# Four edits in the first mixer and the attention of a two-block transformer: a sign step, the input splits, nine modulation columns, and the log-sigmoid rows

## The chip, the cores and the metric

The kernel runs on one core of a Trainium2 chip. The metric is the device time of one execution in microseconds, lower being better. The kernel before takes 2660.37 us (median of 3 runs, 2654.53 to 2660.7).

## The reference, cut to what matters

Two blocks follow each other on a sequence of 512 tokens with 1024 channels. The first block is a stack of two layers, each a mixer and a convolutional gated MLP, with adaptive norms: a vector c gives shift, scale and gate of every norm by a product with a 1024 x 3072 matrix (the "modulation"). The second block is not touched by the change. All is float32.

```python
def adaln_params(c, w, b):                     # shift, scale, gate: 3 x 1024 values
    mod = jax.nn.silu(c) @ w + b
def s5_mixer(h, ...):                          # layer 0
    u = h @ w_in                               # 64 groups of 16 channels, 64 complex states each
    ...                                        # per group: y = scan(bu, lb) through c_re, c_im
    y = jax.nn.gelu(y + d_skip * u)
    y = y * jax.nn.sigmoid(y @ w_glu)
    return y @ w_out
def fox_mixer(h, ...):                         # layer 1, 16 heads
    log_f = jax.nn.log_sigmoid(f_logit + b_f)
    F = lax.cumsum(log_f)                      # one row of 512 per head
    s = q @ k.T + F[t] - F[s]                  # causal, then softmax and p @ v
```

## The kernel before

Channels lie on partitions in eight tiles of 128 x 512 tokens. Each float32 product is three matmuls of rounded halves: high by high, low by high, high by low (`mm3`, L378 to L380). ScalarE (ACT) writes a weight's high half `whi` (L271), VectorE (DVE) or GpSimd (POOL) the low half `wlo` (L272).

**The S5 mixer** takes the first 337 us. Its 64 groups are handled as eight tables of eight groups. For each table n there are steps, each with a letter, and the string ORDER (L76 to L84) writes out by hand in which order they are emitted, and so the order on each of PE, ACT, DVE and POOL; the order on SP's queue, which issues the DMAs, is settled by a list scheduler. W splits an input weight; G is its product with the modulated input, whose result goes out to DRAM (`ud`); F, C, K, R and U build the table (R the rotations on DVE, L924 to L926, C the output weights on POOL, L957 to L959, U two DMAs that turn the rotations into `ecs`); u puts a sign on half of `ecs` (ACT, L987) and writes the decay factors `d` (L990); P transposes (L997, copied to `bp` on ACT, L998); Q makes the lag products (L1006, L1009, copied to `lags` on ACT); A copies them to a Toeplitz tile T with eight DMAs; L loads `ud` back as U; I is the input product (L1027) with two ACT copies (L1030); S multiplies by `ecs`, scans (DVE, L1037 to L1040), copies the halves across (ACT, L1043) and forms `w1` (DVE, L1045); B is L1051 and L1052 on DVE; O the output product (L1060 with T, L1062 with `w1`), a gelu on ACT into `dg` and a DMA to DRAM (`yd`). Y loads `yd` back and splits it into halves, v splits a GLU weight, a and b are GLU matmuls. A round of ORDER, as I call a line of it, has S of table n, P and Q of table n+1, I of table n+1 and O of table n.

**The start.** `split_x(k)` writes the modulated input `hnh` (ACT, L891) and `hnl` (ACT L895 or DVE L893, then DVE L896) of a channel tile. Two of the eight stand ahead of the table powers (`lf`, DVE rows of L721 with ACT copies of L1085 and L1092 between them); the other six are merged among these.

**Modulation columns.** A column of 128 outputs is one 512 KB DMA into a buffer `ada` (L135, two buffers in turn) and one multiply with a sum on DVE (L136). After 16 or 8 columns a bias is added (L151). Columns wait in a list; during a product one or two at a time are taken off at a rate per matmul group, and `need(key)` takes off all that are still before a key's sum. Before the change the list begins behind ORDER, with the 8 gate columns of S5, then 24 for the next norm (`f0`). The eight `z` products after it (`project_out`) apply the gate (L446), and at channel tile 6 of 8 the next norm's `need("f0")` comes.

**The attention of layer 1.** The cumulative sums Fc (16 x 512) are negated to `nF` in two halves, and for each head a matmul with a selector column spreads its row over 128 partitions (L1354), ACT copies it to `b` (L1356), and POOL adds the causal mask to give `bd` (L1358). `scores` adds them to the products on DVE (L575, L578).

Of the kernel before, what the change touches and what calls it, by code (L numbers as in the profile page):

```python
# [9 lines left out]
F32 = mybir.dt.float32  # L10
F32R = mybir.dt.float32r
I32 = mybir.dt.int32
AF = mybir.ActivationFunctionType
OP = mybir.AluOpType
# [4 lines left out]
P = 128  # L19
D = 1024  # L20
S = 512
KD = D // P
# [6 lines left out]
C1 = 6.28125  # L29
C2 = 0.0019350051879882812  # L30
C3 = TWO_PI - C1 - C2
# [21 lines left out]
def _consts():  # L53
# [19 lines left out]
C_DVE, BC_BUFS = 0, 3  # L73
Z_POOL, W_ADD, SUMS_POS, SPREAD_POS, GATE_RATE = 0, 'dve', 12, 22, 1.3
T_ACT, MERGE_AT = 0, 50
ORDER = ("W1 G0 W2 G1 F0 L0 P0 K1 R0 U0 U1 W3 G2 Q0 A0 C1 F1 L1 I0 u0 K2 "  # L76
# [8 lines left out]
LAG_BUFS, U_BUFS, U_ACT, W_DVE, LO_POOL, BC_POS, XR, NORM_POOL, V_DVE, SP_ORDER = 2, 3, 0, 0, 0, 4, 0, 8, 0xaa, 2  # L85
EARLY = 6
BG_AT, BG_RATE = 0, 1.3
# [4 lines left out]
def tile_two_blocks(ctx, tc, ap, out):  # L92
    nc = tc.nc
# [19 lines left out]
    def col(name, i=0, n=1):  # L113
        return vec[:, _OFF[name] + i:_OFF[name] + i + n]
# [7 lines left out]
    def bcast_load(name):  # L122
        t = cst.tile([P, D], F32, name="cb")
        src = ap[name]
        nc.sync.dma_start(t, bass.AP(tensor=src.tensor, offset=src.offset, ap=[[0, P], [1, D]]))
        act.activation(t, t, AF.Silu)
        return t
# [17 lines left out]
    def ada(name, first, cb, m, bias, key, n=24):  # L145

        items = ada_items(name, first, n, cb, m)
        for part, a, b in (("", 0, min(16, n)), ("gate", 16, n)):
            if a < b:
                def done(a=a, b=b, part=part):  # L150
                    dve.tensor_add(m[:, a:b], m[:, a:b], bias[:, a:b])  # L151
                    finished.add(key + part)
                background.extend(items[a:b] + [done])
# [8 lines left out]
    def bg(n):  # L162
        for _ in range(min(n, len(background))):
            background.pop(0)()
# [212 lines left out]
    def mm3(ps, wh, wl, xh, xl, start, stop):  # L377
        pe.matmul(ps, wh, xh, start=start, stop=False)  # L378
        pe.matmul(ps, wh, xl, start=False, stop=False)  # L379
        return pe.matmul(ps, wl, xh, start=False, stop=stop).ins  # L380
# [24 lines left out]
    def bg_rate(r):  # L405
        tick[0] = r
        tick[1] = 0.0
# [315 lines left out]
    def merge(*lists):  # L723

        todo = sorted(((i + 0.5) / len(l), n, i) for n, l in enumerate(lists) for i in range(len(l)))
        for _, n, i in todo:
            lists[n][i]()

    with tc.block(schedule_with_timeline_sim=TIMELINE):
# [156 lines left out]
        def split_x(k):  # L886
            hi, lo = hnp.tile([P, S], F32R, name="hnh"), hnp.tile([P, S], F32R, name="hnl")
            X.append((hi, lo))
            a, b = A[:, k:k + 1], B[:, k:k + 1]
            v = tmp.tile([P, S], F32, name=f"t{k % 4}")  # L890
            act.activation(hi, hs[k], AF.Identity, bias=b, scale=a)  # L891
            if V_DVE >> k & 1:
                dve.tensor_scalar(v, hs[k], a, b, op0=OP.mult, op1=OP.add)  # L893
            else:
                act.activation(v, hs[k], AF.Identity, bias=b, scale=a)  # L895
            (pool if LO_POOL >> k & 1 else dve).tensor_tensor(lo, v, hi.bitcast(F32), OP.subtract)  # L896
# [3 lines left out]
        def split_w(n, eng):  # L900
            t = weights(None, D, eng, raws[n])
            if n + 2 < KD:
                raws.append(load_w(n + 2))
            return t
# [128 lines left out]
        def states(tab, sab):  # L1033

            sa, sb = sab
            z0 = tmp.tile([P, G8, 64], F32, name="t0")
            dve.tensor_mul(z0, sa, tab.ec)  # L1037
            dve.tensor_mul(sb, sb, tab.es)
            dve.tensor_tensor(sa, z0, sb, OP.add)
            dve.tensor_tensor_scan(sa.rearrange("p a b -> p (a b)"), tab.d0.rearrange("p a b -> p (a b)"),  # L1040
                                   sa.rearrange("p a b -> p (a b)"), 0.0, OP.mult, OP.add)
            for a in range(2):
                act.activation(sb[HALF[a]], sa[HALF[1 - a]], AF.Copy, scale=-1.0)  # L1043
            w1 = tmp.tile([P, G8, 64], F32, name="t3")
            dve.tensor_mul(w1, sa, tab.ec)  # L1045
            return w1, sb

        def back(tab, wz):
# [19 lines left out]
                              ys.rearrange("p g n -> p (g n)"))  # L1068

        def load_y(i):  # L1070
            if order.index(i) % 2:
                y = tmp.tile([P, 8, 64], F32, name="sq")
            else:
                y = adp.tile([P, D], F32, name="ada")[:, 0:S].rearrange("p (j n) -> p j n", j=8)
            nc.sync.dma_start(y, yd[i].rearrange("j p n -> p j n"))
            return y.rearrange("p j n -> p (j n)")

# [29 lines left out]
        for x, y, z, op in ((KR, kre, kim, OP.subtract), (KI, kim, kre, OP.add)):  # L1107
            sh = [P, NG, 8]
            t = tmp.tile(sh, F32, name="t0")
            pool.tensor_tensor(x, LR[:, :, 0:8], y[:, :, None].to_broadcast(sh), OP.mult)  # L1110
            pool.tensor_tensor(t, LI[:, :, 0:8], z[:, :, None].to_broadcast(sh), OP.mult)
            pool.tensor_tensor(x, x, t, op)
        dve.tensor_tensor(mod00[:, 0:16].rearrange("p (j i) -> p j i", i=4), ada_ps[:, :, 0::32].rearrange("p i j -> p j i"),
                          col("ada_b", 0, 16).rearrange("p (j i) -> p j i", i=4), OP.add)
        A, B = affine(mod00, 0, 8, col("norm_g", 0, KD), "s5")
        split_x(0)
        split_x(1)
        wt = split_w(0, dve)
        tabs[0].for_c(pool)
        merge([lambda k=k: split_x(k) for k in range(2, KD)], lf.ops)  # L1120
        weights_of, sab, wz, w_of, wg = {0: wt}, {}, {}, {}, {}
        tabs, U = [tabs[0]] + [None] * (KD - 1), [None] * KD
        Y, glu = [None] * KD, {}
# [33 lines left out]
        def do_glu(m, i):  # L1157
            if not i:
                glu[m] = ps_mm.tile([P, S], F32, name="mm")
            k = order[i]  # L1160
            cs_ = slice(k * P, (k + 1) * P)
            mm3(glu[m], wg[m][0][:, cs_], wg[m][1][:, cs_], *Y[k], i == 0, i == KD - 1)
        steps = {
            "K": do_tables, "F": lambda n: tabs[n].for_b(dve), "C": lambda n: tabs[n].for_c(dve if C_DVE >> n & 1 else pool),
            "W": do_w, "G": lambda n: gather(n, weights_of.pop(n)), "P": lambda n: tabs[n].on_pe(), "Q": lambda n: tabs[n].for_lags(), "L": do_u,
            "I": do_inputs, "S": do_states, "B": do_back, "A": lambda n: tabs[n].toeplitz(), "O": do_outputs,
# [7 lines left out]
        scope.close()  # L1174
        zp = scope.enter_context(tc.tile_pool(name="zp", bufs=16))
        bg_rate(GATE_RATE)
        cb1 = bcast_load("c")
        ada("ada_w", 0, cb1, mod00[:, 16:24], col("ada_b", 16, 8), "s5", 8)
        mod01 = cst.tile([P, 24], F32, name="m_ada01")
        mod10 = cst.tile([P, 24], F32, name="m_ada10")  # L1180
        ada("ada_w", 8, cb1, mod01, col("ada_b", 24, 24), "f0")
        ada("ada_w", 32, cb1, mod10, col("ada_b", 48, 24), "fox")
        Z = []
        for m in range(KD):
            if m in glu:
# [128 lines left out]
    pool.memset(one, 1.0)  # L1314
    Fc = ap_.tile([16, S], F32, name="Fc", bufs=1)
    dve.tensor_tensor_scan(Fc, one, pl, 0.0, OP.mult, OP.add)
    nF = ap_.tile([P, S], F32R, name="nF", bufs=1)
    pool.memset(nF.bitcast(F32), 0.0)
    act.activation(nF[0:16], Fc, AF.Copy, scale=-1.0)
    dve.scalar_tensor_tensor(nF[32:48], Fc, -1.0, nF[0:16].bitcast(F32), op0=OP.mult, op1=OP.subtract)  # L1320
    Fq = ap_.tile([P, 4, 16], F32, name="Fq", bufs=1)
    act.activation(Fq, token_major(Fc), AF.Copy)
    sel = ap_.tile([P, 16], F32R, name="sel", bufs=1)
    sel_f = ap_.tile([P, 16], F32, name="sel_f", bufs=1)
    nc.sync.dma_start(sel_f, ap["sel"])
    act.activation(sel, sel_f, AF.Copy)

    mask4 = cc[:, None, 128:256].to_broadcast([P, 4, P])
    Q, K, V = {}, {}, {}
# [1 line left out]
    def qkv_units(wq, wk, wv, X, scale, first):  # L1331
# [16 lines left out]
                units += [lambda i=i, w=wts: uv(i // 2, 0, w), lambda i=i, w=wts: uv(i // 2, 1, w)]  # L1348
        return units

    def fox_head(t, cur):
        i, hh = t // 2, t % 2
        pb = ps_t.tile([P, S], F32, name="pt")
        pe.matmul(pb, sel[:, t:t + 1].to_broadcast([P, P]), nF, start=True, stop=True)  # L1354
        b = tmp.tile([P, S], F32, name="t0")
        act.activation(b, pb, AF.Copy)  # L1356
        bd = tmp.tile([P, S], F32, name="t1")
        pool.tensor_tensor(bd.rearrange("p (a b) -> p a b", a=4), b.rearrange("p (a b) -> p a b", a=4), mask4, OP.add)  # L1358
        cur.scores(Q[i][hh], *K[i][hh], b, bd, 1.0, fq=Fq[:, :, t])
        return V[i // 2]  # L1360

# [359 lines left out]
```

## Time and profile before

| what | value |
|---|---|
| median of 3 runs | 2660.37 us (2654.53 to 2660.7) |
| the profiled execution's own time, and its span | 2663.97 us, 2662.2 us |
| busy time in the span: PE, DVE, ACT, POOL | 2525.7, 1737.6, 1149.0, 359.2 us |
| mean granted clock of TensorE | 0.968 of full |
| PE busy, 102 to 235 us (rounds of S5) | 106.23 of 133 us, clock 0.75 |
| PE busy, 330 to 350 us (end of S5 to the MLP) | 11.92 of 20 us, clock 0.66 |
| PE busy, 740 to 965 us (attention) | 209.19 of 225 us, clock 1.00 |

Busy time of PE alone does not tell where time is lost: at half clock a matmul counts as busy for longer. So clock and busy time are read together, by stretch.

### The profile page before, as it was taken

What the parts mean: (1) busy time and instruction counts of PE and PEld (TensorE: products, weight loads), DVE (VectorE), ACT (ScalarE), POOL (GpSimd) and SP (SyncE); (2) the same over time, 40 slices, a digit from 0 to 9 for tenths busy, and PEclk for the clock granted to TensorE, in tenths of its full rate; (3) what the DMA queues carried; (4) which work ended last, traced back from release to release, by engine and by line L of the source; (5) the groups of instructions that cost most, each with busy time, mean ns of one, the idle gap of its engine ahead of it and who ended that gap; (6) DMA issues with size and microseconds to landing.
All of it is one profiled execution on the core that took longest, in us unless ns stands there. A gap on an engine that the chain in (4) does not pass through costs nothing. (4 is left out here: it accounts for less than half of the span.)

```text
span 2662.2 us, 32825 instructions
## 1 busy us (share of the span) xinstructions
PE 2525.7 (95%) x12098; PEld 2019.1 (76%) x12098; DVE 1737.6 (65%) x3111; ACT 1149.0 (43%) x1925; POOL 359.2 (13%) x346
## 2 busy tenths in 40 slices
PE   5987999999999999999999999999999889999998
PEld 1776778888867777888887777788888667788887
DVE  8764885455586677546567666975767776753554
ACT  3443353233355554323335554532434576542442
POOL 5550000000031110000022110640000220000000
PEclk7877989999999999999999999999999899999999
DMA  5553654444333334455433323545543103223322
GB/s 208 147 131 115 227 185 133 147 138 123 100 120 97 117 122 160 150 177 179 142 101 115 119 92 127 162 148 170 173 138 99 32 29 96 83 88 99 99 79 75
DMA packets 131120, 335.67 MB, mean 126 GB/s; under 512 B 37008, under 2 KB 41872, under 8 KB 130960
## 3 DMA queue, kind: packets, MB, share of 16 engines
q1 hardware_dynamic: 129232, 331.74, 39.6%
q8 instruction: 95, 1.56, 0.2%
q10 hardware_dynamic: 1728, 1.84, 0.2%
q14 instruction: 65, 0.53, 0.1%
HBM read 320.68 MB, written 6.29 MB: 123 GB/s over the span
## 5 line engine op out<-in xcount | busy, mean ns | idle before, releaser
L272 DVE TENSOR_TENSOR wlo<-wraw,whi 128x1024 fp32r<-128x1024 f32 (+4 forms) x424 | 465.1, 1097 | 419.3 <-ACT whi L271 413.6
L271 ACT ACTIVATE whi<-wraw 128x1024 fp32r<-128x1024 f32 (+4 forms) x431 | 407.9, 948 | 748.9 <-PE mm L379 554.3
L378 PE MATMUL mm<-hnh,whi 128*128 128x512 f32 x1152 | 469.3, 408 | 19.3 <-ACT hnh L317 7.5
L379 PE MATMUL mm<-hnl,whi 128*128 128x512 f32 x1152 | 464.7, 404 | 12.4 <-DVE hnl L896 7.5
L380 PE MATMUL mm<-hnh,wlo 128*128 128x512 f32 x1152 | 460.5, 400 | 3.3 <-DVE wlo L272 3.1
L378 PE MATMUL mm<-g,whi 128*128 128x512 f32 (+1 forms) x922 | 359.7, 391 | 6.3 <-ACT g L271 3.1
L380 PE MATMUL mm<-g,wlo 128*128 128x512 f32 (+1 forms) x922 | 359.2, 390 | 0.0
L379 PE MATMUL mm<-g,whi 128*128 128x512 f32 (+1 forms) x922 | 358.9, 389 | 0.1
L378 PE MATMUL s<-hnh,whi 128*128 128x512 f32 x720 | 288.4, 400 | 0.0
L379 PE MATMUL s<-hnl,whi 128*128 128x512 f32 x720 | 285.4, 396 | 0.0
L380 PE MATMUL s<-hnh,wlo 128*128 128x512 f32 x720 | 284.1, 395 | 0.0
L378 PEld LDWEIGHTS mm<-hnh,whi 128*128 128x128 f32 x1152 | 219.7, 191 | 72.9 <-ACT hnh L317 7.9
L379 PEld LDWEIGHTS mm<-hnl,whi 128*128 128x128 f32 x1152 | 219.8, 191 | 71.4 <-DVE hnl L896 11.3
L380 PEld LDWEIGHTS mm<-hnh,wlo 128*128 128x128 f32 x1152 | 219.5, 191 | 54.3 <-DVE wlo L272 5.1
L136 DVE SCALAR_TENSOR_TENSOR ada<-ada,cb 128x1024 f32<-128x1024 f32 x192 | 239.3, 1247 | 9.7 <-DMA ada<-in_ada_w_dram 9.5
L378 PEld LDWEIGHTS mm<-g,whi 128*128 128x128 f32 x922 | 173.5, 188 | 45.4 <-ACT g L271 3.8
L379 PEld LDWEIGHTS mm<-g,whi 128*128 128x128 f32 x922 | 173.9, 189 | 37.7 <-DVE g L277 0.7
L380 PEld LDWEIGHTS mm<-g,wlo 128*128 128x128 f32 x922 | 173.7, 188 | 37.5 <-issue 0.8
L380 PEld LDWEIGHTS s<-hnh,wlo 128*128 128x128 f32 x720 | 135.2, 188 | 32.7 <-issue 0.7
L378 PEld LDWEIGHTS s<-hnh,whi 128*128 128x128 f32 x720 | 135.4, 188 | 30.3
L379 PEld LDWEIGHTS s<-hnl,whi 128*128 128x128 f32 x720 | 135.5, 188 | 29.9 <-issue 0.5
L591 ACT ACTIVATE p<-p,nb 128x128 f32<-128x128 f32 x192 | 105.6, 552 | 69.8 <-DVE nb L586 41.7
(416 smaller groups left out, 3725.8 us busy)
## 6 DMA issues: line engine op xcount, KB each, us to landing
ada<-in_mod_w_dram SPq DMA_DIRECT2D x96, 512.0 KB, 4.2
wraw<-in_ffn_w_up_dram SPq DMA_DIRECT2D x88, 512.0 KB, 3.6
wraw<-in_f_win_dram SPq DMA_DIRECT2D x88, 512.0 KB, 3.5
ada<-in_ada_w_dram SPq DMA_DIRECT2D x80, 512.0 KB, 4.3
wraw<-in_ffn_w_down_dram SPq DMA_DIRECT2D x32, 384.0 KB, 3.1
wraw<-in_f_wout_dram SPq DMA_DIRECT2D x32, 384.0 KB, 3.1
wraw<-in_ffn_w_down_dram SPq DMA_DIRECT2D x32, 320.0 KB, 2.8
wraw<-in_f_wout_dram SPq DMA_DIRECT2D x32, 320.0 KB, 2.8
```

Source lines behind the costliest of these rows:

```text
L136: dve.scalar_tensor_tensor(raw, raw, 1.0, cb, op0=OP.mult, op1=OP.mult, accum_out=dst[:, i:i + 1])
L271: act.activation(hi, v, AF.Copy)
L272: return eng.tensor_tensor(lo, v, hi.bitcast(F32), OP.subtract)
L378: pe.matmul(ps, wh, xh, start=start, stop=False)
L379: pe.matmul(ps, wh, xl, start=False, stop=False)
L380: return pe.matmul(ps, wl, xh, start=False, stop=stop).ins
L591: act.activation(p[:, sl], p[:, sl], AF.Exp, bias=nb[:, qb:qb + 1], scale=scale, accum_out=l[:, qb:qb + 1])
```

## The change

It has four parts. (1) In ORDER the sign step u(n+1) moves from behind O of a round to ahead of the input copies of the same round, and `w1` of S is written ahead of the two ACT copies. (2) At the start the first weight's split and all eight `split_x` come in a row, the table powers after them. (3) A step c loads and activates c and fills the list of columns in round 5 (the line of S5, run after O5), and nine steps g take the eight gate columns of S5 and their bias add in rounds 6 and 7 of ORDER; `yd` is always loaded into a buffer of the name `sq`. (4) The selector matmul, its ACT copy and the low half of `nF` go; `nF` goes to DRAM and each head's row is read back to all 128 partitions by a DMA, for head t and t+1 when head t is emitted.

```diff
-         "S1 W5 F3 B1 U3 C3 P2 G4 Q2 A2 I2 O1 u2 L3 K4 "
+         "S1 W5 F3 B1 U3 C3 P2 G4 Q2 u2 A2 I2 O1 L3 K4 "
...
-         "S5 F7 B5 U7 C7 P6 Q6 A6 I6 O5 Y0 u6 L7 Y1 v0 "
-         "S6 B6 Y2 P7 Q7 A7 a0 a1 I7 O6 u7 Y3 v1 "
+         "S5 F7 B5 U7 C7 P6 Q6 u6 A6 I6 O5 Y0 L7 c0 Y1 v0 "
+         "S6 g0 B6 Y2 g0 P7 Q7 u7 A7 a0 a1 I7 O6 g0 Y3 v1 g0 "
...
+            w1 = tmp.tile([P, G8, 64], F32, name="t3")
+            dve.tensor_mul(w1, sa, tab.ec)
             for a in range(2):
                 act.activation(sb[HALF[a]], sa[HALF[1 - a]], AF.Copy, scale=-1.0)
-            w1 = tmp.tile([P, G8, 64], F32, name="t3")
-            dve.tensor_mul(w1, sa, tab.ec)
...
+        wt = split_w(0, dve)
...
-        split_x(0)
-        split_x(1)
-        wt = split_w(0, dve)
+        for k in range(KD):
+            split_x(k)
         tabs[0].for_c(pool)
-        merge([lambda k=k: split_x(k) for k in range(2, KD)], lf.ops)
+        merge(lf.ops)
...
+        def do_columns(_):
+            bg_rate(0)
+            c_rows.append(bcast_load("c"))
+            cb1 = c_rows[0]
+            ada("ada_w", 0, cb1, mod00[:, 16:24], col("ada_b", 16, 8), "s5", 8)
...
+            "c": do_columns, "g": lambda n: bg(1),
...
-    nF = ap_.tile([P, S], F32R, name="nF", bufs=1)
...
+    nFd = drp.tile([16, S], F32, name="nFd")
+    nc.sync.dma_start(nFd, nF)
...
+    def load_decay(t):
+
+        b = tmp.tile([P, S], F32, name="t0")
+        nc.sync.dma_start(b, nFd[t:t + 1, :].to_broadcast([P, S]))
+        bd = tmp.tile([P, S], F32, name="t1")
+        pool.tensor_tensor(bd.rearrange("p (a b) -> p a b", a=4), b.rearrange("p (a b) -> p a b", a=4), mask4, OP.add)
+        decay[t] = b, bd
...
-        pb = ps_t.tile([P, S], F32, name="pt")
-        pe.matmul(pb, sel[:, t:t + 1].to_broadcast([P, P]), nF, start=True, stop=True)
-        b = tmp.tile([P, S], F32, name="t0")
-        act.activation(b, pb, AF.Copy)
-        bd = tmp.tile([P, S], F32, name="t1")
-        pool.tensor_tensor(bd.rearrange("p (a b) -> p a b", a=4), b.rearrange("p (a b) -> p a b", a=4), mask4, OP.add)
+        for u in range(t, min(t + 2, 16)):
+            if u not in decay:
+                load_decay(u)
+        b, bd = decay[t]
```

On ACT, in the round of O0 (`lags` are the copies of Q1, `s<-s` those of I1, `dg` is O0's gelu, the rows of L987 and L990 are u1), the difference reads:

```order
 L1011 ACTIVATE lags<-pt 16x512 x2
+L987 ACTIVATE ecs<-ecs,cc 128x512
+L990 ACTIVATE d_125<-sm_mag 128x8x63
 L1030 ACTIVATE s<-s 64x512 x2
 L1065 ACT_TABLE_LOAD
 L1065 ACTIVATE dg<-s 128x512
-L987 ACTIVATE ecs<-ecs,cc 128x512
-L990 ACTIVATE d_125<-sm_mag 128x8x63
 L941 ACTIVATE bc<-bc,cc 128x128
```

The sign now stands ahead of the input copies, no longer behind the gelu, which waits for O0's last matmul. The following rounds show the same move.

On DVE at the end of the S5 stage, the last rows of the output products of the kernel before (L446 writes the residual tiles; the pair L151 and L421 forms the next norm's shift and scale, L318 the low halves of the next input):

```order
L136 SCALAR_TENSOR_TENSOR ada,m_ada_1954<-ada,cb 128x1024
L272 TENSOR_TENSOR wlo<-wraw,whi 128x1024
L190 TENSOR_TENSOR sqa<-sqa,sq 128x512
L136 SCALAR_TENSOR_TENSOR ada,m_ada_1954<-ada,cb 128x1024 x2
L446 SCALAR_TENSOR_TENSOR h_98<-mm,m_ada_132,h_98 128x512
L151 TENSOR_TENSOR m_ada_1954<-m_ada_1954,vec 128x16
L421 SCALAR_TENSOR_TENSOR A_f_2498<-m_ada_1954,vec 128x8
```

and in the changed kernel the rows around the third last residual tile:

```order
L318 SCALAR_TENSOR_TENSOR hnl<-h_94,A_f_2498,hnh 128x512
L318 SCALAR_TENSOR_TENSOR hnl<-h_95,A_f_2498,hnh 128x512
L446 SCALAR_TENSOR_TENSOR h_96<-mm,m_ada_132,h_96 128x512
L272 TENSOR_TENSOR wlo<-wraw,whi 128x1024
L136 SCALAR_TENSOR_TENSOR ada,m_ada_606<-ada,cb 128x1024 x2
L190 TENSOR_TENSOR sqa<-sqa,sq 128x512
L318 SCALAR_TENSOR_TENSOR hnl<-h_96,A_f_2498,hnh 128x512
```

The bias add and the scale, which stood behind the last residual tile, now stand ahead of the third last, and five low halves of the next input with them.

On SP in the attention, the changed kernel's first loads (`nFd` is the copy of `nF` in DRAM, `t` the tiles that take a head's row):

```order
L1324 DMA nFd<-nF 16x512
L360 DMA wraw<-in_fox_w_in_dram 128x1024
L1356 DMA t_5729<-nFd 128x512
L1356 DMA t_5733<-nFd 128x512
L360 DMA wraw<-in_fox_w_in_dram 128x1024
L135 DMA ada<-in_ada_w_dram 128x1024
L1356 DMA t_5809<-nFd 128x512
L360 DMA wraw<-in_fox_wv_dram 128x1024
L1356 DMA t_5934<-nFd 128x512
```

Sixteen such loads and one store are new in this queue; they stand among the weights and columns that it issued before.

## Rows read from the trace of the kernel before

**Rows 1.** By stretch: its us, busy us of PE, PEld, DVE, ACT, POOL, clock, DMA.
```profile
102.00:235.00 133.00, 106.23 (x677) 93.48 (x676) 82.40 (x124) 59.67 (x109) 52.20 (x38) 0.75 0.46 116
330.00:350.00 20.00, 11.92 (x43) 9.37 (x42) 18.34 (x45) 6.86 (x12) 0.00 (x0) 0.66 0.63 230
350.00:720.00 370.00, 369.01 (x1608) 298.89 (x1607) 208.84 (x275) 134.42 (x176) 6.98 (x5) 1.00 0.44 138
```

**Rows 2.** The same view, three rounds of S5.
```profile
102.00:120.00 18.00, 17.24 (x111) 15.17 (x110) 16.25 (x23) 9.42 (x18) 10.44 (x7) 0.81 0.48 126
157.00:173.00 16.00, 14.34 (x114) 12.66 (x113) 10.07 (x18) 9.04 (x18) 10.96 (x9) 0.99 0.61 143
195.00:220.00 25.00, 16.03 (x96) 14.26 (x96) 8.59 (x11) 9.94 (x16) 2.53 (x2) 0.56 0.39 96
```

**Rows 3.** PE in order of time, first matmul of outputs O0 and O4.
```profile
101.67 0.43 PE L1060 MATMUL s<-U,T 128*128 128x64 f32 x2 [1.15 <-DVE t L1052]
172.88 0.69 PE L1060 MATMUL s<-U,T 128*128 128x64 f32 x2 [1.66 <-DVE t L1052]
```

**Rows 4.** Who waited for the sign (L987), and for the copies (L1043).
```profile
  DVE s L1038: 13.0, 3
...
  DVE t L1045: 11.6, 8
```

**Rows 5.** DVE in order of time, a rotation beside POOL and after it.
```profile
103.97 1.54 DVE L926 TENSOR_TENSOR ada<-ada,sqa 128x512 f32<-128x512 f32 x1
107.96 0.69 DVE L926 TENSOR_TENSOR ada<-ada,sqa 128x512 f32<-128x512 f32 x1
```

**Rows 6.** The start in order of time: second weight's low half, second gather's copy.
```profile
67.25 2.37 POOL L272 TENSOR_TENSOR wlo<-wraw,whi 128x1024 fp32r<-128x1024 f32 x1 [8.97 <-ACT whi L271]
78.33 0.60 ACT L911 ACTIVATE sq<-mm 128x512 f32<-128x512 f32 x1 [4.78 <-PE mm L380]
```

**Rows 7.** Rounds 5 to 7 in order of time, ACT, PE and DVE.
```profile
180.00 0.60 ACT L1065 ACTIVATE dg<-s 128x512 f32<-128x512 f32 x1 [7.57 <-PE s L1062]
180.50 0.71 ACT L987 ACTIVATE ecs<-ecs,cc 128x512 f32<-128x512 f32 x1
...
182.96 1.28 ACT L126 ACT_TABLE_LOAD   x1 [0.45 <-DMA cb<-in_c_dram]
...
185.59 1.17 ACT L1043 ACTIVATE s<-s 64x512 f32<-64x512 f32 x2
...
187.41 0.58 PE L1006 MATMUL pt<-cp,bt 128*16 128x128 f32 x2 [5.74 <-ACT bp L998]
...
234.69 0.69 PE L1062 MATMUL s<-t,cp 128*128 128x63 f32 x2 [3.35 <-DVE t L1052]
```

**Rows 8.** End of S5 in order of time.
```profile
329.92 0.39 PE L380 MATMUL mm<-z,wlo 128*128 128x512 f32 x1
334.38 1.23 DVE L136 SCALAR_TENSOR_TENSOR ada<-ada,cb 128x1024 f32<-128x1024 f32 x1 [1.25 <-DMA ada<-in_ada_w_dram]
336.20 0.17 DVE L151 TENSOR_TENSOR m_ada<-m_ada,vec 128x16 f32<-128x16 f32 x1
337.77 0.80 PE L378 MATMUL mm<-hnh,whi 128*128 128x512 f32 x1 [7.46 <-ACT hnh L317]
346.00 0.63 PE L380 MATMUL mm<-hnh,wlo 128*128 128x512 f32 x1
```

**Rows 9.** Attention: selector matmuls, who waits for the mask add, and the first score.
```profile
L1354 PE MATMUL pt<-nF,sel x16: 392/398/507, 761.3 to 944.4; 128*128 128x512 f32 x16
...
  DVE p L578: 8.8, 11
...
762.64 0.29 DVE L575 CUSTOM_DVE_ANT_0 p<-s,t 128x128 f32<-128x128 f32 x1 [0.16 <-ACT t L1356]
```

**Rows 10.** DMA issues of 60 to 260 us: KB each, median us to landing.
```profile
U<-ud SPq DMA_DIRECT2D x8, 256.0 KB, 3.7
T<-lags SPq DMA_DIRECT2D x8, 8.0 KB, 1.8
```

More of the change, by code (lines that the diff above doesn't have):

```diff
@@ L75 @@
 T_ACT, MERGE_AT = 0, 50
-ORDER = ("W1 G0 W2 G1 F0 L0 P0 K1 R0 U0 U1 W3 G2 Q0 A0 C1 F1 L1 I0 u0 K2 "
[8 rows of a table removed]
+ORDER = ("W1 G0 W2 G1 F0 L0 P0 K1 R0 U0 U1 W3 G2 Q0 A0 C1 F1 L1 u0 I0 K2 "
[8 rows of a table added]
 LAG_BUFS, U_BUFS, U_ACT, W_DVE, LO_POOL, BC_POS, XR, NORM_POOL, V_DVE, SP_ORDER = 2, 3, 0, 0, 0, 4, 0, 8, 0xaa, 2
@@ L1070, in load_y @@
         def load_y(i):
[L1071 to L1074, printed above, removed]
+            y = tmp.tile([P, 8, 64], F32, name="sq")
             nc.sync.dma_start(y, yd[i].rearrange("j p n -> p j n"))
@@ L1162, in do_glu @@
             mm3(glu[m], wg[m][0][:, cs_], wg[m][1][:, cs_], *Y[k], i == 0, i == KD - 1)
+        mod01 = cst.tile([P, 24], F32, name="m_ada01")
+        mod10 = cst.tile([P, 24], F32, name="m_ada10")
+        c_rows = []
+        def do_columns(_):
[3 more added lines that the diff above has]
+            ada("ada_w", 0, cb1, mod00[:, 16:24], col("ada_b", 16, 8), "s5", 8)
+            ada("ada_w", 8, cb1, mod01, col("ada_b", 24, 24), "f0")
+            ada("ada_w", 32, cb1, mod10, col("ada_b", 48, 24), "fox")
         steps = {
+            "c": do_columns, "g": lambda n: bg(1),
             "K": do_tables, "F": lambda n: tabs[n].for_b(dve), "C": lambda n: tabs[n].for_c(dve if C_DVE >> n & 1 else pool),
@@ L1176, in tile_two_blocks @@
         bg_rate(GATE_RATE)
[L1177 to L1182, printed above, removed]
+        cb1 = c_rows[0]
         Z = []
@@ L1316, in tile_two_blocks @@
     dve.tensor_tensor_scan(Fc, one, pl, 0.0, OP.mult, OP.add)
-    nF = ap_.tile([P, S], F32R, name="nF", bufs=1)
-    pool.memset(nF.bitcast(F32), 0.0)
-    act.activation(nF[0:16], Fc, AF.Copy, scale=-1.0)
-    dve.scalar_tensor_tensor(nF[32:48], Fc, -1.0, nF[0:16].bitcast(F32), op0=OP.mult, op1=OP.subtract)
+    nF = ap_.tile([16, S], F32, name="nF", bufs=1)
+    act.activation(nF, Fc, AF.Copy, scale=-1.0)
+    nFd = drp.tile([16, S], F32, name="nFd")
+    nc.sync.dma_start(nFd, nF)
     Fq = ap_.tile([P, 4, 16], F32, name="Fq", bufs=1)
     act.activation(Fq, token_major(Fc), AF.Copy)
[L1323 to L1326, printed above, removed]
     mask4 = cc[:, None, 128:256].to_broadcast([P, 4, P])
@@ L1349, in qkv_units @@
         return units
+    decay = {}
+    def load_decay(t):
[4 more added lines that the diff above has]
+        decay[t] = b, bd
     def fox_head(t, cur):
         i, hh = t // 2, t % 2
-        pb = ps_t.tile([P, S], F32, name="pt")
-        pe.matmul(pb, sel[:, t:t + 1].to_broadcast([P, P]), nF, start=True, stop=True)
-        b = tmp.tile([P, S], F32, name="t0")
-        act.activation(b, pb, AF.Copy)
-        bd = tmp.tile([P, S], F32, name="t1")
-        pool.tensor_tensor(bd.rearrange("p (a b) -> p a b", a=4), b.rearrange("p (a b) -> p a b", a=4), mask4, OP.add)
+        for u in range(t, min(t + 2, 16)):
+            if u not in decay:
+                load_decay(u)
+        b, bd = decay[t]
         cur.scores(Q[i][hh], *K[i][hh], b, bd, 1.0, fq=Fq[:, :, t])
```

10 rows, old and new, of the table ORDER are left out of this document.

## The prediction

> **What bounds the kernel now.** I read the busy time and the granted clock by stretch first, since busy time alone hides slow matmuls. In the MLP PE is busy for 369 of 370 us at full clock [rows 1]; nothing that this change touches could shorten that. Two stretches differ: the S5 rounds (106 busy of 133 us at clock 0.75) and the 20 us at the end of S5 (11.9 busy at 0.66). There PE waits, and after waits it runs at the lower of its two levels, 1.2 instead of 2.4 GHz. Then, in those stretches, I read PE and the engines that it waits for in order of time, and who waited for the lines that the change moves. The attention is nearly full (209 of 225 us, table).
>
> The rounds from O0 to O4 are four periods in 172.88 - 101.67 = 71.2 us [rows 3], 17.8 us each. One round that PE ran at full clock (157 to 173 us) holds 14.34 us of PE work [rows 2]. So 3.5 us of every round is idle time or low clock. DVE is the engine waited for at O (1.15 and 1.66 us), and DVE itself waited 13.0 us for the sign in three places and 11.6 us for the cross copies in all eight tables [rows 4].
>
> **Part 1, the sign and w1.** No instruction is added; one ACT pair (0.71 us for L987 [rows 7], 1.3 with the `d` copy behind it) moves from behind the gelu, which waits for O's last matmul, to a place ahead of the input copies, where ACT otherwise waits for PE's input product. What is queued behind it there are those copies; the rotated `ecs` it waits for was issued about a round earlier, so I count no new wait. S of the next table then no longer follows O of this one. Can the round fall to PE's 14.3 us? DVE is busy 16.25 us in a round with rotations and 10.07 in one without [rows 2], 13.2 on average, so DVE fits, though without much to spare, since a rotation round's surplus must be made up in the next. I add 1.1 us per round for the O waits of rows 3, which I take to stay in about that size, and get 15.4 us: 4 x (17.8 - 15.4) = **-9.6 us**. Bounds: 0 (another wait takes the place) and 4 x 3.46 = -13.8 (PE full).
>
> Round 5: PE waits 5.74 us for `bp` before Q6 [rows 7]. This is a chain on ACT: O4's gelu at 180.00, the sign at 180.50, four small table copies, the Silu of c with its table load of 1.28 from 182.96 on, the cross copies at 185.59 (1.17), then `bp`. The Silu and its load hold ACT for 2.3 us of it, the sign pair for 1.3. Without them the scan is done before O4 ends, and everything behind the gelu comes 3.6 to 3.7 us sooner: **-3.7**. Round 6: between two Y splits the sign pair (1.3) leaves and load and Silu (2.3) come, in the same chain to Q7: **+1.0**. Round 7: O7's `w1` wait of 3.35 us [rows 7] hangs on DVE; the sign leaves it (-1.3), one column multiply of 1.23 us [rows 8] enters ahead of S7, and `w1` goes beside the cross copies (-0.6): **-0.6**. The rounds: -12.9.
>
> The Trainium skill gives about 2.7 us for a table load (ScalarE: Activation LUTs, Table sets: the hidden batching unit); by that, round 6 would cost 1.4 us more. The row shows 1.28 us here, and I keep it.
>
> **Part 2, the start.** The first gather waits for low halves of input tiles that are merged among the table powers; with all eight splits in a row it ends earlier. But the second gather needs the second weight, whose high half on ACT stands behind copies that wait for the table powers. Before, POOL waited 8.97 us for that half, split the weight from 67.25 on for 2.37 us, and the gather's copy came at 78.33 [rows 6]. The powers now come after all splits instead of between them, so this half moves little: of the work ahead of it only the waits between splits and powers go. I estimate POOL's split 1.5 us and, with a gather that follows the first one closer, the copy 2.5 us sooner: **-2.5**. Bounds: 0, since the scale of the splits now waits for a weight split of about that 2.37 us ahead of it on DVE, and -9 (POOL's whole wait).
>
> **Part 3, nine columns.** The gate columns cost the same DMAs and 1.23 us multiplies, earlier; on DVE they go where it waited for splits and scans in rounds 6 and 7 (8.6 of 25 us busy from 195 to 220 us [rows 2]). At the end the taking-off at the sum has two entries left instead of nine, and the order shows the bias add three residual tiles earlier. In the trace the last `z` product starts at 329.92 + 0.39 to its end, the next PE work at 337.77 after 7.46 us of waiting [rows 8]; the last wait in it is a column's DMA (1.25 at 334.38) and the add at 336.20. PE then runs at half clock until after 346.00: matmuls of 0.63 us instead of 0.39. Half of these nine us is lost, 4.4 us. With high and low halves of five input tiles ready early, both go: -7.46 - 4.4, and I add back 1 us for the statistics, which now come sooner after the last residual tile: **-10.9** (bounds -12 and -5, the latter if the columns before it still come too late). On SP the third and fourth column, which wait for buffers that the first two free, stand ahead of T7's eight DMAs; I count 2 to 3 us of delay there, and T7 has about 8 us to spare ahead of O7.
>
> **Part 4, the decay rows.** Sixteen selector matmuls go, 0.398 us each, at a spacing of 0.23 us 3.7 us of PE [rows 9]; sixteen ACT copies of 0.6 us beside other work cost nothing either way. Against it: the first head. `nF` is written at 759.6; then a store and a load. The nearest rows are 1.8 us for the smallest copy and 3.7 for 256 KB out of DRAM [rows 10], 5.5 in all, plus issues and 1.3 to 2.6 for the mask: the first score, at 762.64, comes near 768, and PE has projections to do meanwhile for most of that. Later heads have their rows a head ahead, some 13 us, against 3.7 + 1.3; the 8.8 us that DVE waited for the mask go, but not on PE's path. I take 3.7 - 2.7 = **-1.0**, between -5 (waits go too) and +6 (start bare).
>
> **The sum.** -12.9 - 2.5 - 10.9 - 1.0 = -27.3 from the profiled execution's own 2663.97 us: 2636.7. The runs shown have a median 3.6 us below that one, which gives 2633.1. I say **2634 us**; the likeliest case's own range is 2619 to 2646.
>
> **Rivals.**
>
> A. *DVE and POOL hold each other up, and rounds stay long.* The same L926 takes 1.54 us while POOL builds output weights and 0.69 after [rows 5]; POOL is busy 10.4 to 11 us of each round [rows 2]. A shorter round puts more of DVE's work beside POOL's. If the round therefore stays at 17.8, the 9.6 go: 2643. Against it: the odd rounds have 10.07 us of DVE beside the same POOL work. The Trainium skill says that a DVE instruction with two SBUF inputs and a GpSimd one that reads SBUF shut each other out for their whole length (SBUF — State Buffer, Who interferes with whom); the two L926 rows agree in direction, and by that rule A is what a round tends to.
>
> B. *The transition's wait is replaced.* The need that popped nine entries goes, but DVE still waits for column DMAs, or the residual tiles come later behind five low halves (0.7 us each) and PE lacks a free PSUM bank. The 10.9 shrink to 2: 2643. With A: 2652.
>
> C. *The rounds' tail wakes up.* If denser work keeps PE at full clock in rounds 5 and 6 (busy 16 of 25 us at 0.56 [rows 2]), up to 8 us more go: 2626. For it, O4 to Q6 get closer; against, Q7 still waits some 9 us.
>
> D. *Slower: decay rows stuck in SP's queue.* A load issued for head t+1 waits for the buffers of head t-1, and the weights and columns behind it wait too; or it stands behind a weight load that waits for a buffer. If each of the 16 heads then exposes more than (27.3 + 8) / 16 = 2.2 us of PE time, the kernel is slower; with 3 us it is 2634 + 48 = 2682. Against it: the loads are small and a head has 13 us.
>
> E. *The edits don't do what they say*: a sign that waits for its turn DMA ahead of the input copies stalls ACT. A wait of 2.4 us in each of the early rounds cancels the gain there; time as in A, and down to 2660 if B holds too.
>
> **How the numbers follow.** Forecast 0.58, A 0.16, B 0.07, C 0.10, D 0.04, E and mixtures of A and B near no change 0.05. What a measurement of this kernel can tell from no change is about 0.3%, 8 us: under 2652.4 it is faster, over 2668.4 slower. Faster 0.90 (forecast, C, most of A and B), same 0.06, slower 0.04. The range of 8 in 10 goes from 2615 (C with the better bound of the rounds) to 2652 (A with B).
>
> **What would show it.** Right: O0 to O4 in about 62 us; no DVE wait for L987; PE wait before Q6 near 2 us; no wait after the last `z` product and full clock at 340 us; second gather's copy near 76. Wrong: periods still near 18 us with DVE rows of 1.5 us; a DMA wait on DVE in the `z` products; DVE or POOL waiting for decay rows in heads after the second.

## The result, and the profile after

The changed kernel takes 2633.02 us (median of 4 runs, 2630.27 to 2637.51) against 2659.13 us (4 runs) for the kernel before: a ratio of 0.990 with a 95% interval of 0.9886 to 0.9913, so 23 to 30 us faster. The forecast was 2634 us. That the sum came out does not mean that its terms did: two of them were off by nearly 5 us each, in opposite directions, and that they cancel is luck.

The table follows the two profiled executions (spans 2662.2 and 2635.6 us) from mark to mark. A mark is the start of a PE instruction, read from PE's rows in order of time.

| from, to | before, us | after, us | gain, us | forecast, us |
|---|---|---|---|---|
| start to O0 | 101.67 | 98.80 | 2.9 | 2.5 |
| O0 to O4 | 71.21 | 66.40 | 4.8 | 9.6 |
| O4 to O5 | 21.93 | 13.57 | 8.4 | 3.7 |
| O5 to O7's first matmul with w1 | 39.88 | 39.05 | 0.8 | -0.4 |
| that to the end of the last z product | 95.62 | 95.62 | 0.0 | 0 |
| to the transposes of the forget gates (fx) | 426.71 | 416.13 | 10.6 | 10.9 |
| to the last attention product | 203.60 | 199.33 | 4.3 | 1.0 |
| to the end of the span | 1701.6 | 1706.7 | -5.1 | 0 |

The last row holds no code that the change touches. In the fourteen profiled executions of this document (twelve experiments, before and after) this stretch takes 1698.7 to 1708.5 us, so -5.1 lies within the spread of single executions and is no effect of the change that could be told; the profiled execution of the changed kernel was the longest of its four runs.

First the stretches of [rows 1] in the profile after (columns as there):

```profile
102.00:235.00 133.00, 101.53 (x709) 88.08 (x708) 97.17 (x144) 62.71 (x114) 52.20 (x38) 0.85 0.59 158
330.00:350.00 20.00, 19.07 (x85) 14.70 (x85) 19.09 (x23) 14.97 (x22) 6.19 (x4) 1.00 0.42 143
350.00:720.00 370.00, 367.46 (x1613) 295.66 (x1613) 205.69 (x286) 129.57 (x173) 8.41 (x9) 1.00 0.42 132
```

PE is busy for less of the 133 us than before although it does more matmuls there (709 instead of 677): the clock is 0.85 instead of 0.75. DVE now works 97 of these 133 us. The 20 us from 330 on are no longer the end of S5, since the kernel is well ahead there, and they show an undisturbed MLP.

PE's waits from Q1 up to O7's `w1` in the profile after, in order of time, with the starts of O0 to O5 between them (98.80, 119.76, 133.89, 151.06, 165.20, 178.77); two waits of 1.40 and 0.53 us for a GLU weight, behind O6, are left out:

```profile
94.73 0.38 PE L1006 MATMUL pt<-cp,bt 128*16 128x128 f32 x2 [1.67 <-ACT bp L998]
98.80 0.39 PE L1060 MATMUL s<-U,T 128*128 128x64 f32 x2
113.58 0.59 PE L1006 MATMUL pt<-cp,bt 128*16 128x128 f32 x2 [4.65 <-ACT bp L998]
119.76 0.39 PE L1060 MATMUL s<-U,T 128*128 128x64 f32 x2
133.89 0.39 PE L1060 MATMUL s<-U,T 128*128 128x64 f32 x2
147.00 0.38 PE L1006 MATMUL pt<-cp,bt 128*16 128x128 f32 x2 [2.98 <-ACT bp L998]
151.06 0.39 PE L1060 MATMUL s<-U,T 128*128 128x64 f32 x2
165.20 0.39 PE L1060 MATMUL s<-U,T 128*128 128x64 f32 x2
173.35 0.59 PE L1006 MATMUL pt<-cp,bt 128*16 128x128 f32 x2 [3.54 <-ACT bp L998]
178.77 0.39 PE L1060 MATMUL s<-U,T 128*128 128x64 f32 x2
195.17 0.59 PE L1006 MATMUL pt<-cp,bt 128*16 128x128 f32 x2 [11.78 <-ACT bp L998]
217.82 0.69 PE L1062 MATMUL s<-t,cp 128*128 128x63 f32 x2 [4.55 <-DVE t L1052]
```

The waits for t ahead of O0 to O4 of [rows 3] are gone, and no instruction waits for the sign any more ([rows 4] had 13.0 us). But the rounds are unequal: 20.96 us from O0 to O1, then 14.13, 17.17, 14.14. The odd rounds run at PE's speed. The two longer ones are those with rotations, and the wait in them is for `bp`. Only one of these waits is new, the 4.65 us ahead of Q2. The kernel before had none there, but it waited for `bp` ahead of Q1 (1.05 us), Q4, Q6 ([rows 7]) and Q7:

```profile
151.37 0.38 PE L1006 MATMUL pt<-cp,bt 128*16 128x128 f32 x2 [2.92 <-ACT bp L998]
212.52 0.58 PE L1006 MATMUL pt<-cp,bt 128*16 128x128 f32 x2 [8.97 <-ACT bp L998]
```

ACT, DVE and POOL in the first of the long rounds after tell why:

```profile
101.17 1.53 DVE L926 TENSOR_TENSOR ada<-ada,sqa 128x512 f32<-128x512 f32 x1
102.12 1.61 POOL L958 TENSOR_TENSOR op<-LI,bc 128x576 f32<-128x576 f32 x1
102.63 1.65 DVE L924 TENSOR_TENSOR ada<-cb 128x512 f32<-128x512 f32 x1
103.81 1.76 POOL L959 TENSOR_TENSOR cp<-cp,op 128x576 f32<-128x576 f32 x1
104.20 1.92 DVE L925 TENSOR_TENSOR sqa<-cb 128x512 f32<-128x512 f32 x1
106.16 0.69 DVE L926 TENSOR_TENSOR ada<-ada,sqa 128x512 f32<-128x512 f32 x1
...
110.08 0.69 DVE L1043 TENSOR_TENSOR t<-s,ecs 128x512 f32<-128x512 f32 x1
...
110.81 1.17 ACT L1045 ACTIVATE s<-s 64x512 f32<-64x512 f32 x2 [6.44 <-DVE t L1043]
111.91 1.04 ACT L271 ACTIVATE whi<-wraw 128x1024 fp32r<-128x1024 f32 x1
112.85 1.06 ACT L998 ACTIVATE bp<-pt 128x512 f32<-128x512 f32 x2
```

The rotations, beside POOL, take 8.7 us (98.04 to 106.77; about 4.2 alone). Each of the five that meet POOL ends 0.54 or 0.55 us after the POOL instruction that was under way when it began (104.28 after 103.73, 106.12 after 105.57). S1 comes behind them on DVE; the cross copies of S1 wait for it on ACT for 6.44 us, and `bp`, whose transposes PE had ended at 103.4, stands behind those and a weight split. Also, the copies start when `w1` has ended (110.08 + 0.69), not when the scan has.

The end of S5 after, against [rows 8], PE and DVE in order of time:

```profile
297.57 0.17 DVE L151 TENSOR_TENSOR m_ada<-m_ada,vec 128x16 f32<-128x16 f32 x1
...
313.05 0.39 PE L380 MATMUL mm<-z,wlo 128*128 128x512 f32 x1
313.27 0.40 PE L378 MATMUL mm<-hnh,whi 128*128 128x512 f32 x1
313.51 0.40 PE L379 MATMUL mm<-hnl,whi 128*128 128x512 f32 x1
```

The bias add is done 15 us ahead of the last z product, PE goes on without a wait, and at full clock. In the attention, against [rows 9], the first score waits for its row now:

```profile
740.45 0.29 DVE L575 CUSTOM_DVE_ANT_0 p<-s,t 128x128 f32<-128x128 f32 x1 [2.43 <-DMA t<-nFd]
```

It comes 10.88 us after the fx transposes (729.57), where it was 5.62. The view of DMA issues has 1.6 us for the store of `nF` and 3.3 us in the middle for a row.

### The profile page after: what moved, and what is told of

Same layout as the page of the kernel before. It is cut to its first block, busy times and chain, and to the rows that moved or that the text cites. A ratio compares the mean times of both kernels' runs of the same rounds, so it can differ in the third digit from the quotient of the medians.

```text
span 2635.6 us, 32802 instructions
## 1 busy us (share of the span) xinstructions
PE 2506.6 (95%) x12082; PEld 2004.9 (76%) x12082; DVE 1742.7 (66%) x3110; ACT 1140.0 (43%) x1908; POOL 357.5 (14%) x345
## 5 line engine op out<-in xcount | busy, mean ns | idle before, releaser
L478 ACT ACTIVATE t<-t 128x512 f32<-128x512 f32 x88 | 55.5, 631 | 185.9 <-DVE t L455 176.5
```

Source lines behind the costliest of these rows:

```text
L478: act.activation(sa, ya, AF.Silu)
```

## The experiments

All ratios are against runs of the kernel before on the same chip in the same session; the changed kernel's own is 0.9900 (0.9886 to 0.9913). Medians of different sessions differ by a microsecond or two, and the medians of single kernels have 4 to 8 runs, so I read differences under 4 us from the traces only, by marks. Marks have a spread of their own, since each kernel has one trace: from the last z product to fx the same code takes 413.3 to 417.1 us in the twelve kernels that have its columns early.

### The four parts, each undone alone

```diff
 # no_sign: ORDER
-... G4 Q2 u2 A2 I2 O1 L3 K4
+... G4 Q2 A2 I2 O1 u2 L3 K4      (every round; w1 behind the copies)
 # no_start
+        split_x(0); split_x(1); wt = split_w(0, dve)
...
+        merge([lambda k=k: split_x(k) for k in range(2, KD)], lf.ops)
 # no_cols: ORDER without c0 and the nine g0, and behind it
+        do_columns(0); bg_rate(GATE_RATE)
 # no_decay: selector matmul, ACT copy, nF in two halves as before
```

> The changed kernel with part 1 alone undone: every sign step back behind its round's output product, w1 back behind the cross copies; start, columns and decay rows as changed. Theory (the parts act in places of their own and add up, and part 1 made the 14.0 us by which O0 to O7 came closer together, 133.0 to 119.0 us): about 2633 + 13 = 2646 us, O0 to O7 near 132 us with the DVE waits for L987 back at some 13 us. Rival (the shorter rounds come from the columns and the moved Silu in the tail, and the sign only shifts waits): at most 2638 us, O0 to O7 under 124 us.

Measured: 2649.47 us, 0.9957 (0.9941 to 0.9972), its runs spread from 2641 to 2657. In the trace O0 to O7's `w1` takes 137.2 us, and DVE's wait for L987 is back in three places with 15.0 us. The theory was right, and its number a little small. (The trace is of an execution of 2657.28 us.)

> The changed kernel with part 2 alone undone: two input splits ahead of the first weight, the other six merged among the table powers again. Theory: the start is worth what O0 moved, 2.9 us (101.67 to 98.80), so 2636 us, with the second gather's copy back near 78.3 us. Rival (the rounds after it are bound by a chain of their own and take up the start's gain): 2633 us.

Measured: 2638.44 us, 0.9924 (0.9909 to 0.9938). The second gather's copy is late again, O0 starts at 100.94, 2.1 us behind the changed kernel. But O7's first matmul comes 6.6 us later (219.37 against 212.75). The rival expected the rounds to absorb the difference; in this trace they enlarged it. The windows of 114 to 172 us, first the changed kernel and then this one, show by what:

```profile
114.00:172.00 58.00, 52.84 (x423) 47.00 (x421) 49.76 (x75) 31.52 (x63) 39.01 (x29) 0.96 0.63 160
```
```profile
114.00:172.00 58.00, 54.13 (x386) 48.43 (x386) 45.22 (x71) 30.35 (x59) 37.91 (x27) 0.85 0.56 147
```

PE is busy for longer and does fewer matmuls: the granted clock is 0.85 in place of 0.96. After the wait for `bp` (4.68 us, as in the changed kernel) its matmuls stayed at the slow level until 131 us. In the changed kernel that stretch had ended by 119 us. This is one trace, and its whole span is no longer than the changed kernel's (2634.8 and 2635.6 us), since behind the attention, where the code is the same, it took 8.1 us less. By the medians the part is worth 5.4 us.

> The changed kernel with part 3 alone undone: the Silu of c and the nine entries come after the hand-written order again; sign, start and decay rows as changed. Theory: the wait of 7.5 us after the last output product and the half clock behind it come back, and rounds 6 and 7 lose one Silu and some column multiplies: 2633 + 11 = 2644 us, PE waiting 7 us for hnh there. Rival (the columns cost as much in rounds 6 and 7 as they save at the end): 2633 to 2636 us.

Measured: 2642.26 us, 0.9936 (0.9921 to 0.9952). The wait is back, in this row of PE:

```profile
318.33 0.80 PE L378 MATMUL mm<-hnh,whi 128*128 128x512 f32 x1 [4.50 <-ACT hnh L317]
```

It is 4.5 us and not 7.5, but from the last z product to fx this kernel needs 423.9 us against 416.1: 7.8 us with the half clock that follows (matmuls of 0.63 to 0.80 us until 329 us). O7's `w1` matmul comes 1.9 us sooner without the columns, but that is lost again before the last z product, which ends 0.4 us later than in the changed kernel. So up to fx part 3 is worth 8.2 us; the theory's sign and place hold, its 11 us were too much by a quarter.

> The changed kernel with part 4 alone undone: the selector matmul, its ACT copy and the two halves of nF are back, no row goes through DRAM. Theory from the two traces: up to the attention the changed kernel is 27.4 us ahead (transpose of fx at 757.02 against 729.57), at the end of the span 26.6, so the decay rows by DMA cost about 0.8 us: 2632 us. Rival (the prediction's step): they save 1 us, 2634 us.

Measured: 2635.7 us, 0.9906 (0.9891 to 0.9921), no difference from the changed kernel that can be told. Both numbers in the expectation fit that. From fx to the last attention product the selector needs 203.3 us here (203.6 in the kernel before), the decay rows 199.3. The twelve kernels with the decay rows need 198.4 to 204.0 us there, with a median of 200.6, so the rows save about 3 us. The spans of this pair are equal all the same (2635.7 and 2635.6), so in this pair 4 us are lost later. Aligned matmul by matmul, 1.6 us go at once, in the next norm. The 10 us from 970 on, with the selector and then with the decay rows:

```profile
970.00:980.00 10.00, 10.00 (x61) 8.75 (x60) 6.95 (x23) 2.31 (x3) 0.00 (x0) 1.00 0.57 194
```
```profile
970.00:980.00 10.00, 10.00 (x51) 8.50 (x50) 5.25 (x21) 1.06 (x1) 0.00 (x0) 0.83 0.32 108
```

PE is busy throughout in both, and in the second at 0.83 of the clock; neither trace shows a wait of PE ahead of it. The decay rows are not what brings this about: counted from the last attention product, the same stretch runs at a clock of 1.00 in the other thirteen traces, eleven of them with the decay rows. So the loss belongs to this one execution. Why the clock fell in it stays open.

### Where the rounds' missing gain went

```diff
 # p_first, every round
-S1 W5 F3 B1 U3 C3 P2 G4 ...
+P2 S1 W5 F3 B1 U3 C3 G4 ...
 # w1_back (p_w1: both)
             for a in range(2):
                 act.activation(sb[HALF[a]], sa[HALF[1 - a]], AF.Copy, scale=-1.0)
+            w1 = tmp.tile([P, G8, 64], F32, name="t3")
+            dve.tensor_mul(w1, sa, tab.ec)
 # c_memset, in step C
-                for a in (0, 4): ... six POOL multiplies and adds
+                eng.memset(cp, 0.01)
```

> The changed kernel with P of the next table moved ahead of S in every round of ORDER, so that on ACT the bp copies stand ahead of S's cross copies and the weight split; nothing else. Theory (after the change PE's waits for bp, 1.67 + 4.65 + 2.98 + 3.54 + 11.78 = 24.6 us, are only a matter of ACT's order: bt was ready a round earlier): these waits go; O and the later rounds then wait for DVE, which takes about half back: 2633 - 12 = 2621 us, the 11.78 us ahead of Q7 under 3. Rival (DVE with its rotations beside POOL bounds the rounds, and PE would wait for t at O instead): 2630 to 2634 us.

Measured: 2633.33 us, 0.9894 (0.9873 to 0.9916): nothing. The waits for `bp` fell from 24.6 to 5.5 us as expected, and O0 to O1 from 20.96 to 18.82 us. But O1 now starts within 0.1 us of the end of DVE's t, so that S1, F and B hold it:

```profile
106.74 0.68 DVE L1037 TENSOR_TENSOR t<-s,ecs 128x512 f32<-128x512 f32 x1
...
116.25 0.69 DVE L1052 TENSOR_TENSOR t<-t,s 128x512 f32<-128x512 f32 x1
...
117.04 0.59 PE L1060 MATMUL s<-U,T 128*128 128x64 f32 x2 [1.27 <-ACT s L1030]
```

The profile puts the wait down to the input copies, which ended at 117.04; t was ready at 116.94, so even without them O1 could have come only 0.1 us sooner. The rival was right: with `bp` out of the way DVE bounds the round, and a half-clock stretch between O1 and O2 (19.02 us at a mean clock of 0.73) took what was left.

> The changed kernel with w1 of S written behind the cross copies again, the signs as changed. Theory from the trace after (a cross copy now starts when w1 ends, 110.81 after 110.08 + 0.69, not when the scan ends): the swap delays bp by 0.7 us in rounds where PE waits for bp, and brings t 0.6 us sooner where it waits for t, so it is worth nothing: 2632 to 2635 us. Rival (the prediction's step, 0.6 us in round 7 alone, and more in rounds that wait for t): 2636 us or more.

Measured: 2642.78 us, 0.9924 (0.9898 to 0.9950), with three of six runs near 2647 us, two near 2632.7 and one between. The waits ahead of O0 are as the theory had them: `bp` 0.94 us in place of 1.67, and t 1.15 in place of none. What the theory left out is the clock. PE waits 1.15 us for t ahead of O3 too, the round behind it runs at a clock of 0.73 (19.03 us instead of 14.14), and O7's `w1` comes 6.3 us later than in the changed kernel (224.15). This trace is of one of the three long runs; two of six are as fast as the changed kernel, and the interval meets that of the changed kernel. So whether the swap is worth 0 or 9 us is not settled, and with it how much of part 1 is the sign's.

> P ahead of S and w1 behind the cross copies, both. Theory: with P early the cross copies no longer delay bp, so that where w1 stands matters only for t; w1 back costs 0.6 us in a round that waits for t: 0 to 4 us above the run with P ahead alone. Rival (copies first also let B start sooner): 0 to 4 us below it.

Measured: 2639.23 us, 0.9922 (0.9898 to 0.9946), 6 us above the run with P ahead alone by the medians. The sign is the theory's, the size above it, and the intervals touch.

> The changed kernel in which POOL fills the output weights cp with a constant (one memset instead of the six multiplies and adds of step C), so the S5 outputs are not computed: POOL's reads beside DVE's rotations are taken away, DVE's own work is unchanged. Rival A of the prediction (POOL's work beside the rotations holds DVE up and that sets the rotation rounds): rotations of 4.2 instead of 8.7 us, O0 to O1 from 20.96 to 16.5 us, O2 to O3 from 17.2 to 15, 2633 - 8 = 2625 us. Rival (the rounds hang on ACT's order alone): rotations shorter, O0 to O1 above 19 us, 2630 us or more.

Measured: 2619.06 us, 0.9844 (0.982 to 0.9867). Every round from O0 to O4 takes 14.14 us (94.90, 109.04, 123.17, 137.31, 151.45), and the rotations of the first on DVE read:

```profile
94.15 0.68 DVE L924 TENSOR_TENSOR ada<-cb 128x512 f32<-128x512 f32 x1
94.75 0.69 DVE L925 TENSOR_TENSOR sqa<-cb 128x512 f32<-128x512 f32 x1
95.47 0.69 DVE L926 TENSOR_TENSOR ada<-ada,sqa 128x512 f32<-128x512 f32 x1
```

Without POOL's reads they take 0.69 us each, and the rounds run at PE's speed with ACT's order unchanged. Rival A of the prediction was true of the rotation rounds, and only of those. The gain is larger than either theory's because the first gathers come 4 us earlier too: POOL also holds up the low halves of the input (L896), two of which in a row take 3.04 us beside it in the changed kernel and 0.69 each here.

### Putting POOL's work elsewhere, and the rest of the chain

```diff
 # c_early (and p_f_c0_ce), rotation rounds
-S0 W4 F2 B0 R1 U2 C2 P1 ...
+S0 C2 W4 F2 B0 R1 U2 P1 ...
 # p_f_c0: P ahead of S; F's first two multiplies as a step f of its own
-S1 W5 F3 B1 ...
+P2 S1 W5 f3 B1 F3 ...
-Q6 u6 A6 I6 O5 Y0 L7 c0 Y1 v0
+Q6 u6 A6 I6 c0 O5 Y0 L7 Y1 v0
 # tail, on p_f_c0_ce
-I6 c0 O5 Y0 L7 Y1 v0 | P7 S6 g0 B6 Y2 g0 ... O6 g0 Y3 v1 g0 | S7 g0 B7 Y4 g0
+I6 c0 O5 P7 S6 Y0 L7 Y1 v0 | B6 Y2 g0 g0 ... O6 S7 Y3 v1 | B7 g0 Y4 g0 ... (two g more behind O7)
```

> The changed kernel with step C of rotation rounds moved ahead of the weight split (C2, C4, C6 right behind S0, S2, S4), so that POOL's output weights run beside DVE's F and no longer beside the rotations; no work is left out. Theory (the round is held by DVE's rotations beside POOL's reads, as the run with cp filled by a constant showed with 14.14 us for every round): if F does not suffer from the same neighbour, rotations fall from 8.7 to 4.2 us and O0 to O1 from 20.96 to about 17 us, 2633 - 6 = 2627 us. Rival (every DVE instruction with two inputs in SBUF suffers, F too): F grows by what the rotations lose, O0 to O1 above 19.5 us, 2631 to 2637 us.

Measured: 2628.37 us, 0.9869 (0.9843 to 0.9895). O0 to O1 falls to 15.29 us (97.35 to 112.64). F does not suffer at all, while the first rotation waits for POOL's weight split. DVE and POOL in order of time:

```profile
93.10 0.42 DVE L974 TENSOR_TENSOR bt<-bt,aux 128x256 f32<-128x256 f32 x1
93.15 1.17 POOL L958 TENSOR_TENSOR op<-LI,bc 128x576 f32<-128x576 f32 x1
93.55 0.43 DVE L972 TENSOR_TENSOR aux<-KI,aux 128x256 f32<-128x256 f32 x1
...
95.76 2.37 POOL L272 TENSOR_TENSOR wlo<-wraw,whi 128x1024 fp32r<-128x1024 f32 x1
96.60 2.07 DVE L924 TENSOR_TENSOR ada<-cb 128x512 f32<-128x512 f32 x1
98.59 0.68 DVE L925 TENSOR_TENSOR sqa<-cb 128x512 f32<-128x512 f32 x1
```

L924 ended 0.5 us after POOL's split did and needs 0.69 alone: it stood still for nearly all of the overlap. F's L972 and L974 keep their 0.43 us with POOL busy beside them. The Trainium skill's rule that the prediction weighed (SBUF — State Buffer, Who interferes with whom) names a DVE instruction with two inputs in SBUF. The rotations read two; L972 and L974 do not, since `aux` is a tile in PSUM, the memory that PE writes its results to (pool `ps_a`, L105; L1079 of the kernel before, L1076 of the changed one). So the rule fits both, and the rival was wrong to count F among such instructions: of the 48 single L972 and L974 rows in the rounds of the changed kernel 40 overlap POOL, and all 48 take 0.42 or 0.43 us. Of the 8.9 us by which O4 comes earlier here than in the changed kernel (156.26 and 165.20), 5.7 are lost again up to O7's `w1` (214.59 and 217.82): PE's clock from O4 to O6 is 0.73 and 0.54 here, 0.87 and 0.72 there.

> The changed kernel with three moves, no work left out: P of the next table ahead of S; the first two multiplies of F ahead of B and the rest behind it, so that O waits for less of DVE; the Silu of c between I6 and O5, beside PE's output product. Theory (bp behind the cross copies, t behind F and the Silu in round 6 are three links of the chains that are left): O1 about 4 us earlier than the 117.04 of the run with P ahead alone, Q7 2 us earlier, 2633 - 10 = 2623 us. Rival (the rotation rounds are bound by DVE beside POOL whatever the order): 2629 to 2634 us.

Measured: 2621.6 us, 0.9846 (0.9817 to 0.9875). O1 starts at 113.78 (117.04 with P ahead alone), and from O5 to O7's first matmul 26.9 us pass instead of 34.0. The theory holds.

> The same three moves, and C of rotation rounds ahead of the weight split besides. Theory: the gains add if F does not suffer beside POOL: 2618 us, O0 to O4 under 60 us. Rival: C beside F delays bt and with it bp, 2625 us or more.

Measured: 2615.34 us, 0.9822 (0.9797 to 0.9847), the runs from 2613.4 to 2617.1. O0 to O4 takes 56.9 us, 14.2 a round, and from 102 to 150 us PE is busy for 47.91 of 48 us at full clock. By the medians this is some 18 us under the changed kernel and 44 under the kernel before, with no work left out.

> The fastest run so far (P ahead of S, F split around B, the Silu beside O5, C of rotation rounds early) with the last two rounds put in another order: P7 and S6 right behind O5 and ahead of the Y splits, S7 right behind O6, and the column steps g behind S and B; no work left out. Theory (in the trace of that run O7's w1 wait of 5.96 us hangs on DVE, where S7 stood behind the splits of Y3 and v1 and a column whose DMA was waited for 1.75 us): the wait goes and S6 fills 3.1 us in which DVE waited, 2615 - 6 = 2609 us. Rival (the GLU products then wait for their splits instead, since ACT and DVE do the same work in another order): 2613 to 2617 us.

Measured: 2615.26 us, 0.9818 (0.9792 to 0.9843), no difference, and the runs spread more (2607 to 2620). O7's wait for `w1` (5.96 us) is gone, but the GLU products wait for their halves instead (2.60, 1.36 and 1.35 us), and the last z product ends 1.5 us later. The rival was right.

## Why the prediction was right, point by point

**The total** was right to 1 us, and the closeness is luck: the sign and the bound of each of the four parts held, but within part 1 O0 to O4 gained 4.8 us less than forecast and round 5 4.7 us more.

**The sign** (9.6 us forecast for O0 to O4, 4.8 measured) failed at one step. "DVE fits, though without much to spare, since a rotation round's surplus must be made up in the next": it cannot be made up, since S of the next table stands behind the rotations, and the rotations themselves grew from 7.1 to 8.7 us as more of POOL's work fell beside them. What the prediction had as rival A, for all rounds, holds for the rotation rounds; c_memset shows it, and the 14.13 us of the other rounds show that 15.4 was too much there. And "I count no new wait" missed one: the cross copies wait on ACT ahead of `bp`, and PE with them for 4.65 us ahead of Q2. What the part did gain is clock: from O0 to O4 PE's busy time fell from 65.3 to 58.8 us, while its idle time rose from 5.9 to 7.6 us.

**Round 5** (3.7 forecast, 8.4 measured): the chain was read rightly, but what it frees was oversized: the wait ahead of Q6 fell by 2.2 us, from 5.74 to 3.54, not by 3.7. The other 6.2 us are clock: from O4 to O5 it was 0.87 instead of 0.50, and PE was busy for 10.03 us instead of 16.19. That is rival C, which the sum left out. **Rounds 6 and 7** came out 0.8 us better, not 0.4 worse, and by C again: the Silu sits in the chain as forecast (load at 183.68 for 1.28 us), PE's wait ahead of Q7 grew from 8.97 to 11.78 us (1.0 forecast), and a clock of 0.72 instead of 0.56 from O5 to O6 made up for it. In p_f_c0, where the Silu stands beside O5 along with two other moves, O5 to O7 is 7.1 us shorter; the Silu's share was not measured alone.

**The start** came out as forecast (2.9 us at O0 for 2.5, the second gather's copy at 76.16). What the prediction did not have is that such a difference can grow: without part 2 it was 6.6 us at O7 in the one trace, by a longer stretch at half clock.

**The columns**: the end of S5 gave 10.6 us of the forecast 10.9, by the mechanism named, the wait and then the half clock. Alone (no_cols) the part is worth about 9 us by the medians and 8.2 by the marks up to fx, since without it the wait is shorter than before the change. The delay that I had counted for T7 on SP did not come: its DMAs were issued from 199.85 us on, when its lags were copied (199.80).

**The decay rows**: the 5.3 us for the first score were right (10.88 instead of 5.62 after fx), and so was it that PE had work meanwhile: the attention as a whole gained 4.3 us in this pair and about 3 by the median of the kernels with the rows, near the 3.7 us of the selector matmuls, so that little of the 2.7 us that I had set against it shows. POOL did wait for rows, 128.9 us in 14 heads, which the prediction had named as a sign of being wrong. It cost nothing that shows, since DVE waited only 0.6 us for a mask (8.8 before) and, in the first head, 2.4 us for a row. Rivals B, D and E did not occur.

## What to carry to other kernels

In a hand-ordered pipeline, look past the wait that a move removes to what then stands first on each in-order engine: here `bp` stood behind copies that were late, with its own input long ready, and PE waited 4.65 us for it where it had not waited before. Before shortening a round, sum each engine's work in the longest round and not in the mean, and add what two engines do to each other when more of their work falls side by side; look up in which memory each input lies, since here that told the instructions that were held up from those that were not. And count a stall of TensorE with the stretch at half clock that follows it: a wait of 7.46 us cost 10.6 here, and one of 4.50 us 7.8.

## What the runs showed of the hardware that I had not expected

- POOL's output-weight and weight-split instructions hold up the rotations, which read two inputs in SBUF: L924 takes 2.07 us instead of 0.69 and ends 0.54 us after POOL's split. Instructions of the same kind with one of the two inputs in PSUM go on beside POOL unchanged (L972 at 0.43 us beside L958).
- The granted clock fell to 0.83 for 10 us behind the attention in one of fourteen traces, with PE busy throughout and no wait ahead of it.
- A small delay ahead of a tight loop may grow: in one trace 2.1 us at O0 became 6.6 us at O7, with the clock from 114 to 172 us at 0.85 in place of 0.96.
